# Turned values and keys through DRAM, and sums made by accumulating transfers, in a planned one-core decoder layer

## The chip, the cores and the metric

The kernel runs on one core of one Trainium2 chip. The metric is the device time of one execution in microseconds (us), lower is better. Three timed runs of the kernel before gave 276.04, 276.61 and 276.85 us, so the median is 276.61 us. The engines are named as in the profile: PE does matrix products (and transposes, as products with an identity matrix), DVE works on vectors, ACT evaluates functions and scales, POOL also does vector work and issues transfers, SP only issues transfers.

## The reference, cut to what matters

```python
h = x @ w_in                                  # x: (512, 1024) prompt rows and 8 decode rows
qa, ka, va, za, ga, qb, kb, vb, gb = split(h)
# mixer A, 4 heads, dk=64, dv=128: S_t = diag(a_t) S_{t-1} + k_t^T v_t, o_t = q_t S_t, in chunks
new_state = exp(b_last) * state + einsum('bhsd,bhsv->bhdv', k * exp(b_last - b), v)
# decode rows, one token each: new_state = a * state + k^T v
# mixer B, 8 heads of 64: windows (128,1), (512,4), (2048,16) over past keys, merged by denominators
mix = concat(o_a * silu(ga), o_b * silu(gb))
y = mix @ w_out
out = layer_norm(alpha * x + y, ln_g, ln_b)   # alpha = sqrt(2)
```

Outputs are both groups' rows, the states of mixer A after prompt and decode step, and the new key and value rows. All is float32.

## The kernel before, in words

**Who sets the order.** Every piece of work is a Python generator that yields operations one by one. A planner (class `Plan`, lines 85 to 381, its loop `run` in lines 312 to 334) holds an estimate of every engine's time, takes the generator whose next operation could start first, and among equals the one with the lowest rank, the number given in `add(generator, rank)`. `dense()` at rank 100 is the main stream of projections. What comes out is a fixed order for each engine; on the chip each engine goes through its row in order and waits where an operand isn't there. All instructions are recorded at one line (380 before, 382 in the changed kernel), so groups are told apart by tiles. `SLOTS` and `BANKS` say how many buffers each pool has, `ORDER` in which order the weight groups come, `QUEUE` which engine issues a named kind of transfer ("D" is SP, "G" is POOL).

**Projections.** Every float32 product is made of three passes with operands split into a high and a low part (hi·hi, lo·hi, hi·lo). A weight group has 256 columns. Groups that `token` makes (lines 704 to 721: the values `vb0`, `vb1`, `va0`, `va1`) come for the first two token tiles with features on the partitions (`f`=0, 1; 264 columns, 256 prompt tokens and the 8 decode rows) and for the last two with tokens on the partitions. Attention wants tokens there, so the first half has to be turned. `turn` (730 to 738) does it: a copy to SBUF, two transposes on PE, and a copy from PSUM.

**Keys of mixer A.** `gla_state` (1019 to 1071) makes the decayed keys `kd` (two feature halves, 512 tokens), turns them by eight PE transposes into two PSUM tiles `ps_kt`, copies them to `kt`, and later multiplies `kt` with the values (`ps_kv`).

**Decode state.** `sample_state` (1522 to 1542) works in two halves of four sequences: the old state `s4` comes by SP, ACT multiplies eight 128x128 pieces by the decay, and DVE adds value times key to each (`scalar_tensor_tensor`, 16 in all). SP stores the sum.

**Output.** `out_first` (1764) makes the first two token tiles of the output projection with features on the partitions, four groups g of 256 features. `out_turn` turns them. For g = 3 this is done on PE. For g = 0, 1, 2 the route goes through DRAM: ACT copies `ps_yf` to `feat_y`, DVE turns 32x32 blocks of it into `yw` (`blocks`, 740), POOL stores `yw` to the DRAM tensor `ysc` (`store_blocks`), and POOL loads it back turned into `yx` (`load_turned`). Then `out_evac` (1827) forms y = alpha·y + yx on DVE for token tiles 0 and 1, where y holds the input rows, and takes statistics with `bn_stats` pieces of 256 columns. When all four groups of a tile are in, `norm` (1874) combines statistics, subtracts the mean and multiplies by gamma on DVE, gets 1/sqrt on ACT and DVE, multiplies and adds beta, and stores. Tiles 2 and 3 (`y2`, `y3`) come with tokens on the partitions straight from PE; `y3` is last, and its 512-, 256- and 256-column pieces end the kernel (`last_norm`, 1721). The decode rows have their own small norm (`w_s`, `sums_s`, `residual_sample`), in which PE sums the rows (`ps_ms`, `ps_vs`).

Of the kernel before, what the change touches and what calls it, by code (L numbers as in the profile page):

```python
# [17 lines left out]
ALU = mybir.AluOpType  # L18
# [48 lines left out]
SLOTS = dict(g=23, w=7, r=3, sv=5, pt=2, far=5, tp=2, vp=2, t2=2, st=3, pr=4, t1=5, ob=3, m=6)  # L67
# [11 lines left out]
QUEUE = dict(y="G")  # L79
SLOW, SHARE = 1100, 1.7  # L80

ORDER = "qa0 qb0 qb1 qb2 qb3 kb0 kb1 vb0 kb2 kb3 gb0 vb1 gb1 va0 gb2 gb3 va1 ga0 ga1 ga2 ga3".split()


class Op:
# [3 lines left out]
    def __init__(self, eng, fn, args, kw):  # L89
# [5 lines left out]
        if "accum_out" in kw:  # L95
            self.writes.append(kw["accum_out"])
        if fn == "tensor_tensor_reduce":
            self.writes.append(self.reads.pop())
# [286 lines left out]
def trunk(ctx: ExitStack, tc: tile.TileContext, xT, xp, xs, state, ck, cv, w_in, wab, gnorm,  # L385
# [24 lines left out]
    def rsqrt(o, x, scale, eps, between=None):  # L410
# [4 lines left out]
        if between:  # L415
# [3 lines left out]
            add(between, 5)  # L419
# [284 lines left out]
    def token(g, evac_f, evac):  # L704

        for f in range(2):
# [6 lines left out]
            add(evac_f(ps, f), 61.9)  # L713
# [35 lines left out]
    def load_turned(q, out, sc):  # L749
        return q.dma_start(out, sc.rearrange("k p j -> p k j"))  # L750

# [52 lines left out]
    def dense():  # L804
# [28 lines left out]
        add(gate_decay(pz), 19.1)  # L833
# [10 lines left out]
        add(residual_sample(), 19.7)  # L844
# [82 lines left out]
    def gla_levels():  # L927
# [6 lines left out]
        for li, h in enumerate(LEVELS):  # L934
# [25 lines left out]
            if li % 2:  # L960
                add(gla_level(made), 46.7)
                made = []
# [56 lines left out]
    def gla_state():  # L1019
# [53 lines left out]
    def gla_queries():  # L1073
# [12 lines left out]
        for u in range(2):  # L1086
            yield from make(f"oa{u}", Need("g", f"oa{u}", [P, 2, 512]), 2)
            add(gla_out(u), 13.3 + u)

    def gla_out(u):  # L1090
# [30 lines left out]
        for i in range(2):  # L1121
            add(gla_head(u, i, ps, po), 26 + u + i / 2)
# [17 lines left out]
    def parts(n, own, m, scale):  # L1140

        def evac(ps, u):
# [20 lines left out]
            if n == "k":  # L1163
                add(keys_out(ps, m, u), 9.7)
# [357 lines left out]
    def sample_state():  # L1522
        yield At("vat_out")
        for i in range(2):
# [8 lines left out]
            for bb in range(4):  # L1533
                bi = i * 4 + bb
                for m in range(2):
# [3 lines left out]
            yield D.dma_start(st_s[i * 4 * 256:(i + 1) * 4 * 256, :].rearrange("(b p) v -> p b v", p=P),  # L1539
                              s4.rearrange("p b m v -> p (b m) v"))  # L1540
# [129 lines left out]
    def residual(t):  # L1670
# [7 lines left out]
        yield D.dma_start(y, xp[t * P:t * P + P, :])  # L1678
        mark(f"y{t}")
# [60 lines left out]
    def out_unit(t, c, w, seeded=None):  # L1740
# [16 lines left out]
        if seeded is not None:  # L1757
            add(last_norm(t, ps), 48.2)
        elif w == GW + 2:
            add(early_mean(t, ps), 2)  # L1760
        else:
            add(out_evac(t, c // GW, ps[:, :w]), 2.9)

    def out_first(*units):
# [6 lines left out]
        for (g, f), p in zip(units, ps):  # L1771
            yield from out_half(g, f, p, range(4, KT))
            add(out_turn(g, f, p), 0.3)
# [11 lines left out]
    def out_turn(g, f, ps):  # L1785
        if g == 3:
# [13 lines left out]
            if plan.marks[f"yt_in{g}"] == 2:  # L1800
                plan.share(B[f"yt{g}"], 2)
                for t in range(2):
                    add(out_evac(t, g, B[f"yt{g}"][:, t * GW:t * GW + GW]), 40.9)
# [13 lines left out]
        if plan.marks[f"yt_in{g}"] == 2:  # L1817
# [3 lines left out]
            yx = yield Need("g", f"yx{g}", [P, 2, GW])  # L1821
            yield load_turned(queue["y"], yx.rearrange("p t (k j) -> p (t k) j", j=32), ysc[g])
            plan.share(yx, 2)
            for t in range(2):
                add(out_evac(t, g, yx[:, t]), 2)

    def out_evac(t, g, ps):
# [3 lines left out]
        yield V.scalar_tensor_tensor(y[:, c], y[:, c], ALPHA, ps, op0=ALU.mult, op1=ALU.add)  # L1831
# [201 lines left out]
```

## Time and profile before

| | before |
|---|---|
| median of three timed runs | 276.61 us |
| the profiled execution's own time | 276.23 us |
| its span, first to last instruction | 274.3 us |
| granted PE clock, mean | 0.994 |
| busy: PE / DVE / ACT / POOL | 264.2 / 220.6 / 157.9 / 64.0 us |
| packets moved, bytes | 62999, 54.67 MB |

The profile is one execution. Its time is 1.9 us more than its span, since something lies ahead of the first and behind the last recorded instruction. A row of a group gives engine, operation, output and input by the program's names (buffer numbers left out), shapes, count, then busy time, mean ns of one, idle time ahead of them and who ended most of it. Durations on PE are longer than the distance between starts, since its instructions overlap. The chain of waits is followed back from the last instruction: at each step to what released it.

### The profile page before, as it was taken

The numbers are of one execution on the slowest core, as the hardware profiler recorded it, in microseconds if no ns is written. First come the engines' busy times: TensorE is split into PE (matmuls) and PEld (weight loads), VectorE is DVE, ScalarE is ACT, GpSimd is POOL, SyncE is SP. The second block draws the span as 40 slices with busy tenths as digits, with TensorE's granted clock in tenths as the row PEclk, the third lists the DMA queues.
The fourth block names the chain that finished last, engine by engine and source line by source line (L and its number), as shares of the span: only waits on it lengthen the run. The fifth ranks groups of instructions, "written<-read, shape, count | busy, mean of one in ns | idle before, by whom it ended". The sixth has DMA issues, their size and how long they took to land.

```text
span 274.3 us, 7448 instructions
## 1 busy us (share of the span) xinstructions
PE 264.2 (96%) x2869; PEld 248.9 (91%) x2869; DVE 220.6 (80%) x584; ACT 157.9 (58%) x478; POOL 64.0 (23%) x77
## 2 busy tenths in 40 slices
PE   8999999999799999999999999999999999999990
PEld 5999999899799999989998989999999999998890
DVE  5746789998989799988499954965989898448995
ACT  4727856565457676686464754735589975420221
POOL 3000000000576538220054435353200001330000
PEclk9999999999999999999999999999999999999997
DMA  6978948327959968737599999897952485896142
GB/s 212 342 192 196 301 130 226 81 76 210 307 172 278 236 206 273 194 84 203 153 223 279 282 219 272 217 206 162 244 159 76 114 290 144 228 282 192 58 171 81
DMA packets 62999, 54.67 MB, mean 199 GB/s; under 512 B 13933, under 2 KB 55059, under 8 KB 62965
## 3 DMA queue, kind: packets, MB, share of 16 engines
q1 hardware_dynamic: 61909, 52.18, 69.4%
q0 software_dynamic: 480, 1.57, 2.2%
q8 instruction: 22, 0.36, 0.5%
q10 hardware_dynamic: 576, 0.46, 0.5%
q14 instruction: 12, 0.10, 0.1%
HBM read 47.26 MB, written 7.73 MB: 200 GB/s over the span
## 4 chain that ended last, share of the span: by engine, by line
PE 80%; DMA 8%; DVE 6%; issue 2%; SPq 1%; POOL 0%; ACT 0%; DVEq 0%; POOLq 0%
PE ps_kb L380 9%; PE ps_ga L380 9%; PE ps_gb L380 9%; PE ps_qb L380 9%; PE ps_vb_f L380 4%; PE ps_va_f L380 4%; PE ps_vb L380 4%; PE ps_va L380 4%; PE ps_qa L380 4%; DMA ysc<-yw 4%; PE ps_yf L380 4%; DVE y L380 4%; PE ps_pv L380 3%; PE ps_s L380 3%; PE ps_ka L380 3%; DMA yx<-ysc 3%
## 5 line engine op out<-in xcount | busy, mean ns | idle before, releaser
L380 POOL TENSOR_TENSOR past<-past,qbc 128x256 f32<-128x256 f32 x32 | 29.0, 939 | 86.2 <-DMA qbc<-qsd 77.5
L380 POOL TENSOR_TENSOR vv<-vv,pb 128x256 f32<-128x256 f32 x32 | 26.8, 867 | 48.9 <-DMA pb<-psd_s 43.2
L380 ACT ACTIVATE pr<-pr,ms 128x128 f32<-128x128 f32 (+3 forms) x48 | 23.0, 493 | 7.8 <-DVE ms L380 7.8
L380 ACT COPY pt<-ps_pt 128x256 f32<-128x256 f32 (+1 forms) x29 | 9.8, 347 | 10.4 <-PE ps_pt L380 10.2
L380 DVE CUSTOM_DVE_ANT_0 pr<-ps_s,strip 128x128 f32<-128x128 f32 (+3 forms) x32 | 11.5, 407 | 3.9 <-PE ps_s L380 3.8
L380 ACT ACTIVATE sg<-sg 128x264 f32<-128x264 f32 (+1 forms) x32 | 13.7, 429 | 0.6
L380 PE MATMUL ps_ka<-xx,hi_ka 128*128 128x264 f32 (+1 forms) x64 | 12.2, 283 | 0.0
L380 POOL DMA_DIRECT2D ysc<-yw x3 | 2.5, 818 | 41.0 <-DVE yw L380 40.6
L380 PE MATMUL ps_pt<-cf,pr 128*128 128x128 f32 x56 | 11.3, 274 | 0.0
L380 DVE TENSOR_REDUCE lt<-past 128x8 f32<-128x512 f32 x16 | 10.5, 668 | 0.0
L380 PEld LDWEIGHTS ps_ka<-xx,hi_ka 128*128 128x128 f32 x64 | 9.9, 190 | 0.1
L380 DVE TENSOR_REDUCE o_pv<-vv 128x4 f32<-128x1024 f32 x8 | 9.7, 1206 | 0.0
L380 ACT ACTIVATE d<-d 128x512 f32<-128x512 f32 x11 | 6.6, 641 | 3.9 <-DVE d L380 3.8
L380 PE MATMUL ps_ka<-xx,lo_ka 128*128 128x264 f32 (+1 forms) x32 | 8.7, 283 | 0.0
L380 ACT ACTIVATE qh<-ps_qb 128x128 fp32r<-128x128 f32 x16 | 5.2, 438 | 5.9 <-PE ps_qb L380 5.8
L380 ACT COPY feat_y<-ps_yf 128x256 f32<-128x256 f32 x8 | 3.0, 373 | 8.9 <-PE ps_yf L380 8.9
L380 DVE TENSOR_TENSOR far<-tp,same 128x128 f32<-128x128 f32 (+1 forms) x16 | 8.1, 526 | 0.0
L380 DVE STREAM_TRANSPOSE yw<-feat_y 128x256 f32<-128x256 f32 x6 | 3.8, 640 | 4.8 <-ACT feat_y L380 4.7
L380 PE MATMUL ps_qa<-xx,hi_ka 128*128 128x264 f32 (+1 forms) x32 | 7.4, 304 | 0.1
L380 ACT CAST mhb<-gb 128x256 fp32r<-128x256 f32 x8 | 3.2, 405 | 7.2 <-DVE gb L380 7.2
L380 PEld LDWEIGHTS ps_pt<-cf,pr 128*128 128x128 f32 x56 | 6.9, 140 | 0.3 <-ACT hi_gb__2144 L380 0.2
L380 DVE TENSOR_TENSOR gb<-ps_gb,sg 128x256 f32<-128x256 f32 x8 | 3.4, 419 | 4.4 <-ACT sg L380 4.1
(574 smaller groups left out, 1079.1 us busy)
## 6 DMA issues: line engine op xcount, KB each, us to landing
past<-in_ck_dram SPq DMA_DIRECT2D x8, 512.0 KB, 4.7
vv<-in_cv_dram SPq DMA_DIRECT2D x8, 512.0 KB, 7.2
pb<-psd_s SPq DMA_DIRECT2D x16, 256.0 KB, 7.1
s<-in_state_dram SPq DMA_DIRECT2D x4, 512.0 KB
qbc<-qsd SPq DMA_DIRECT2D x8, 256.0 KB, 5.4
y<-in_xp_dram SPq DMA_DIRECT2D x4, 512.0 KB
x_raw<-in_xT_dram SPq DMA_DIRECT2D x6, 260.0 KB, 5.9
out_dram<-y SPq DMA_DIRECT2D x3, 512.0 KB
```

Of the source, the lines that this page charges most:

```text
L380: getattr(eng.eng, op.fn)(*op.args, **op.kw)
```

## The change

Five things are edited, and nearly every rank is another number.

- **Values of mixer B, first half.** No PE transposes (eight go): `rows_of` copies to SBUF, turns 32x32 blocks on DVE into `vbw`, and after the second feature half SP stores to a DRAM tensor `vsc` and loads back turned into `v0` or `v1`.
- **Decayed keys.** The eight PE transposes and their two ACT copies go. Two DVE block transposes of 128x512 into `kx`, a store to `ksc` and a turned load into `kt`, both issued by POOL.
- **Decode state.** The 16 DVE operations go. ACT multiplies value pieces by the key too (16 more multiplications); SP stores the decayed old state, and POOL adds the products to it in DRAM by an accumulating transfer.
- **Turned outputs.** The load into `yx` and the DVE sum go for g = 0, 1, 2. y0 and y1 are multiplied by alpha once, on ACT, when they are loaded. From `ysc` POOL issues two accumulating transfers per group, one into y0 and one into y1. For g = 3 DVE adds without the factor.
- **Statistics of y2.** DVE's four `bn_stats` and one aggregation become two ACT passes of 1024 columns with accumulated sums (`sq2`, from pool "r").

Pool "w" has 8 buffers for 7 and "sv" 4 for 5; in `ORDER`, `va1` and `gb3` change places.

```diff
-SLOTS = dict(g=23, w=7, r=3, sv=5, pt=2, far=5, tp=2, vp=2, t2=2, st=3, pr=4, t1=5, ob=3, m=6)
+SLOTS = dict(g=23, w=8, r=3, sv=4, pt=2, far=5, tp=2, vp=2, t2=2, st=3, pr=4, t1=5, ob=3, m=6)
-QUEUE = dict(y="G")
+QUEUE = dict(y="G", v="D", k="G")
...
+    def rows_of(g, f, ps):
+        yield from make(f"vbw{g}", Need("g", f"vbw{g}", [P, 2, 2, P])) if f == 0 else iter((At(f"vbw{g}"),))
+        w = B[f"vbw{g}"]
+        feat = yield Need("t1", "feat", [P, GW])
+        yield copy(feat, ps[:, :GW])
+        free(ps)
+        yield blocks(w[:, :, f], feat)
+        free(feat)
+        if f:
+            yield store_blocks(queue["v"], vsc[g], w.rearrange("p t f c -> p (t f) c"))
+            free(w)
+            yield load_turned(queue["v"], B[f"v{g}"][:, :2, :].rearrange("p t (k j) -> p (t k) j", j=32), vsc[g])
+            for _ in range(2):
+                mark(f"vb{g}")
...
+        kx = yield Need("g", "kx", [P, 2, NP])
+        for m in range(2):
+            yield blocks(kx[:, m].rearrange("p (c t) -> p c t", c=TT), kd[:, m])
+        free(kd)
+        yield store_blocks(queue["k"], ksc, kx.rearrange("p m (c t) -> p (m c) t", c=TT))
+        free(kx)
         kt = yield Need("g", "kt", [P, 2, TT, P])
-        for m in range(2):
-            ps = yield bank("t", "ps_kt")
-            for c in range(TT):
-                yield T.transpose(ps[:, c * P:c * P + P], kd[:, m, c * P:c * P + P], ident)
-            yield copy(kt[:, m].rearrange("p c t -> p (c t)"), ps)
-            free(ps)
-        free(kd)
+        yield load_turned(queue["k"], kt.rearrange("p m c (a j) -> p (m c a) j", j=32), ksc)
...
-            ps, raw = yield from turn(ps)
-            free(raw)
-            yield copy(B[f"v{i}"][:, :2, f * P:f * P + P], ps[:, :GW].rearrange("p (t c) -> p t c", t=2))
-            free(ps)
-            mark(f"vb{i}")
+            yield from rows_of(i, f, ps)
...
-                    yield S.mul(s4[:, bb, m, :], s4[:, bb, m, :], a_s[:, m, bi:bi + 1])
-                    yield V.scalar_tensor_tensor(s4[:, bb, m, :], v4[:, bb, m, :], ka_s[:, m, bi:bi + 1], s4[:, bb, m, :],
-                                                 op0=ALU.mult, op1=ALU.add)
...
+            for x, scale in ((s4, a_s), (v4, ka_s)):
+                for bb in range(4):
+                    for m in range(2):
+                        yield S.mul(x[:, bb, m, :], x[:, bb, m, :], scale[:, m, i * 4 + bb:i * 4 + bb + 1])
+                x = x.rearrange("p b m v -> p (b m) v")
+                yield D.dma_start(to, x) if scale is a_s else G.dma_start(to, x, accum_op=ALU.add)
...
-            yx = yield Need("g", f"yx{g}", [P, 2, GW])
-            yield load_turned(queue["y"], yx.rearrange("p t (k j) -> p (t k) j", j=32), ysc[g])
-            plan.share(yx, 2)
             for t in range(2):
-                add(out_evac(t, g, yx[:, t]), 2)
+                yield At(f"y{t}")
+                yield G.dma_start(B["y", t][:, g * GW:g * GW + GW].rearrange("p (k j) -> p k j", j=32),
+                                  ysc[g][8 * t:8 * t + 8].rearrange("k p j -> p k j"), accum_op=ALU.add)
+                add(out_stats(t, g, 1), 9.2)
...
+        if t in (2,):
+            sq = yield Need("r", f"sq{t}", [P, DM])
+            yield S.activation(sq, y, AF.Identity, accum_out=mv[:, 0:1])
+            yield S.mul(mean, mv[:, 0:1], -1.0 / DM)
+            yield S.activation(sq, y, AF.Square, bias=mean, accum_out=mv[:, 1:2])
+            free(sq)
...
-    add(gla_levels(), 20.3)
+    add(gla_levels(), 12.1)
```

**Three places in the new order.** First, POOL's row at the end of the program, before. `vv` and `pb` are past values of the decode rows, `yw0` to `yw2` the turned blocks, `ysc` their DRAM tensors:

```order
L380 TENSOR_TENSOR vv7_3010<-vv7_3010,pb7_3063 128x256 x4
L380 DMA ysc0_95<-yw0_3878 128x4x128
L380 DMA ysc1_96<-yw1_3921 128x4x128
L380 DMA yx0_3918<-ysc0_95 128x16x32
L380 DMA ysc2_97<-yw2_3957 128x4x128
L380 DMA yx1_3953<-ysc1_96 128x16x32
L380 DMA yx2_4004<-ysc2_97 128x16x32
```

POOL's row at the same place in the changed kernel; `out_3_dram` is the decode state in DRAM and `v40`, `v41` are the products of its two halves:

```order
L382 DMA out_3_dram<-v40_3486 128x8x128
L382 DMA ysc0_95<-yw0_3875 128x4x128
L382 DMA ysc1_96<-yw1_3910 128x4x128
L382 DMA y0_3706<-ysc0_95 128x8x32
L382 DMA y1_3708<-ysc0_95 128x8x32
L382 DMA y0_3706<-ysc1_96 128x8x32
L382 DMA y1_3708<-ysc1_96 128x8x32
L382 DMA ysc2_97<-yw2_3952 128x4x128
L382 DMA out_3_dram<-v41_3813 128x8x128
L382 DMA y0_3706<-ysc2_97 128x8x32
L382 DMA y1_3708<-ysc2_97 128x8x32
```

The store of `yw2` stood behind one turned load; now it stands behind four accumulating transfers, which wait for the landings of the first two stores, and the transfer of `v41` stands between it and the last two.

Second, DVE's row near the end, before, with what each instruction waits for (DMASW are POOL's transfers, DMAHW SP's):

```order
L380 SCALAR_TENSOR_TENSOR y2_4042<-y2_4042,ps_y20_4079 128x512 [waits DMAHW1_49,DMASW0_49,PE_49]
L380 BN_STATS stats2_4043<-y2_4042 128x6 [waits DVE_49]
L380 BN_STATS stats2_4043<-y2_4042 128x6
L380 COPY sums_s_85<-ps_ms_4118 64x1 [waits PE_49]
L380 TENSOR_SCALAR w_s_3730<-w_s_3730,sums_s_85 64x128 [waits DVE_49]
L380 SCALAR_TENSOR_TENSOR y0_3726<-y0_3726,yx2_4004 128x256 [waits DMASW5_49]
L380 SCALAR_TENSOR_TENSOR y1_3728<-y1_3728,yx2_4004 128x256
L380 BN_STATS stats0_3727<-y0_3726 128x6 [waits DVE_49]
L380 BN_STATS stats1_3729<-y1_3728 128x6 [waits DVE_49]
L380 BN_AGGR mv0_4152<-stats0_3727 128x2 [waits DVE_49]
```

The same place in the changed kernel:

```order
L382 SCALAR_TENSOR_TENSOR y2_4035<-y2_4035,ps_y20_4068 128x512 [waits DMAHW6_49,PE_49]
L382 COPY sums_s_85<-ps_ms_4105 64x1 [waits PE_49]
L382 TENSOR_SCALAR w_s_3710<-w_s_3710,sums_s_85 64x128 [waits DVE_49]
L382 BN_STATS stats0_3707<-y0_3706 128x6 [waits DMASW3_49]
L382 BN_AGGR mv0_4133<-stats0_3707 128x2 [waits DVE_49]
L382 TENSOR_SCALAR newton_4139<-mv0_4133 128x1 [waits DVE_49]
L382 SCALAR_TENSOR_TENSOR y0_3706<-y0_3706,mv0_4133,gamma_4042 128x1024 [waits DMAHW0_49]
L382 BN_STATS stats1_3709<-y1_3708 128x6 [waits DMASW4_49]
```

DVE's wait for the last load of `yx` has become a wait for the accumulating transfer into y0, at the statistics that stand ahead of all three norms; the statistics of y2 are gone from its row, and the wait for y1 comes behind the first big operation of y0.

Third, PE's row where the decayed keys were turned, before (`ps_kb2_0` is a dense product, `ps_pt31` a turned probability tile):

```order
L380 MATMUL ps_kb2_0_1588<-xx0_132,lo0_kb2__1386 128x264
L380 MATMUL ps_kt_1567<-cf_66,kd_1408 128x128 x4
L380 MATMUL ps_kb2_0_1588<-xx0_132,hi0_kb2__1230 128x264
L380 MATMUL ps_kb2_0_1588<-xx0_133,hi0_kb2__1230 128x264
L380 MATMUL ps_kb2_0_1588<-xx0_132,lo0_kb2__1386 128x264
L380 MATMUL ps_kb2_0_1588<-xx2_215,hi0_kb2__1230 128x264
L380 MATMUL ps_pt31_1584<-cf_66,pr30_1332 128x128 x2
```

And PE's row in the changed kernel where the turned values are first used (`ps_pv00`, the weighted values of mixer B):

```order
L382 MATMUL ps_vb1_2_1968<-hi1_vb1__1734,xx6_309 128x256
L382 MATMUL ps_rows_1987<-cf_66,vnt_82 32x128
L382 MATMUL ps_pv00_2014<-pt00_1284,v0_1364 64x256 x2
L382 MATMUL ps_pv00_2014<-pt10_1473,v0_1364 64x256 x2
L382 MATMUL ps_pv00_2014<-pt00_1284,v0_1364 64x128 x2
L382 MATMUL ps_pv00_2014<-pt10_1473,v0_1364 64x128 x2
L382 MATMUL ps_pt02_2036<-cf_66,pr02_1583 128x128 x2
L382 MATMUL ps_vb1_3_2015<-hi0_vb1__1682,xx0_132 128x256
```

There is no `ps_kt` in the changed row. The first product with `v0` stood within the last third of `kb2`'s first half; now it stands inside `vb1`, 264 dense products behind the end of `vb0`'s feature-major half.

More of the change, by code (lines that the diff above doesn't have):

```diff
@@ L418, in rsqrt @@
             yield S.activation(o, o, AF.Exp, scale=-0.5)
-            add(between, 5)
+            add(between, 24.1)
             yield S.activation(t, o, AF.Square)
@@ L832, in dense @@
         free(zw, *xraw)
-        add(gate_decay(pz), 19.1)
+        add(gate_decay(pz), 41.3)
         yield from make("ka", Need("g", "ka", [P, 2, NP]), 3)
@@ L843, in dense @@
             add(residual(t), 10.3)
-        add(residual_sample(), 19.7)
+        add(residual_sample(), 40.8)
         units = [(g, f) for g in range(4) for f in range(2)]
@@ L960, in gla_levels @@
             if li % 2:
-                add(gla_level(made), 46.7)
+                add(gla_level(made), 62.4)
                 made = []
@@ L1121, in gla_out @@
         for i in range(2):
-            add(gla_head(u, i, ps, po), 26 + u + i / 2)
+            add(gla_head(u, i, ps, po), 51.1 + u + i / 2)
     def gla_head(u, j, ps, po):
@@ L1163, in evac @@
             if n == "k":
-                add(keys_out(ps, m, u), 9.7)
+                add(keys_out(ps, m, u), 56.4)
             else:
@@ L1772, in out_first @@
             yield from out_half(g, f, p, range(4, KT))
-            add(out_turn(g, f, p), 0.3)
+            add(out_turn(g, f, p), 10.7)
     def out_half(g, f, ps, ks):
@@ L1830, in out_evac, with out_stats @@
         c = slice(g * GW, g * GW + size(ps))
-        yield V.scalar_tensor_tensor(y[:, c], y[:, c], ALPHA, ps, op0=ALU.mult, op1=ALU.add)
+        if t < 2:
+            yield V.tensor_tensor(y[:, c], y[:, c], ps, op=ALU.add)
+        else:
+            yield V.scalar_tensor_tensor(y[:, c], y[:, c], ALPHA, ps, op0=ALU.mult, op1=ALU.add)
         free(ps)
-        for i in range(g, g + size(ps) // GW):
-            yield V.bn_stats(st[:, i, :], y[:, i * GW:i * GW + GW])
+        yield from out_stats(t, g, size(ps) // GW)
+    def out_stats(t, g, n):
+        y, st = B["y", t], B["stats", t]
+        for i in range(g, g + n):
+            if t not in (2,):
+                yield V.bn_stats(st[:, i, :], y[:, i * GW:i * GW + GW])
             mark(f"y{t}_done")
```

84 lines of the change are left out of this document (44 added, 40 removed).

## The prediction

> **What bounds the kernel now.** I read the page first (span and busy time), then what PE waits for, then the last 42 us by windows, then the chain of waits and DVE's and PE's timelines at the end. The page's first lines and PE's waits, with the time in total, the times and the longest:
>
> ```profile
> span 274.3 us, 7448 instructions
> PE 264.2 (96%) x2869; PEld 248.9 (91%) x2869; DVE 220.6 (80%) x584; ACT 157.9 (58%) x478; POOL 64.0 (23%) x77
> PE ps_kb L380 <- issue: 1.5, 1, 1.5
> PE warm_ps L380 <- DVE warm L1892: 1.2, 1, 1.2
> PE ps_og L380 <- issue: 0.7, 1, 0.7
> ```
>
> PE is busy 264.2 of 274.3 us. Inside its stream there are two holes worth a name, 1.5 and 0.7 us, and behind neither stands another engine. So time is PE's stream plus what follows its last product. The windows hold length, then busy time (and instructions) of PE, PEld, DVE, ACT and POOL, the granted clock, the DMA share and GB/s:
>
> ```profile
> 232.00:240.00 8.00, 8.00 (x68) 8.00 (x68) 3.29 (x8) 3.29 (x14) 3.19 (x4) 1.00 0.90 239
> 240.00:247.00 7.00, 7.00 (x50) 6.51 (x50) 3.24 (x11) 1.71 (x7) 2.74 (x3) 1.00 1.04 283
> 254.00:261.00 7.00, 7.00 (x33) 5.67 (x32) 6.97 (x17) 1.85 (x11) 0.00 (x0) 1.00 0.18 75
> 261.00:268.00 7.00, 6.61 (x53) 6.27 (x51) 6.93 (x24) 1.83 (x9) 0.00 (x0) 1.00 0.36 150
> ```
>
> From 254 to 268 two engines are full at once: PE without a gap until its end, and DVE 6.97 and 6.93 of 7. In the windows ahead of these the transfers are full instead (0.90 and 1.04). How the two meet, in rows of DVE's, PE's and ACT's timelines (start, length, what):
>
> ```profile
> 251.72 0.13 DVE L380 COPY sums_s<-ps_ms 64x1 f32<-64x1 f32 x1
> 252.70 0.76 DVE L380 SCALAR_TENSOR_TENSOR y<-y,yx 128x256 f32<-128x256 f32 x2 [0.53 <-DMA yx<-ysc]
> 264.95 0.40 DVE L380 SCALAR_TENSOR_TENSOR y<-y,ps_y 128x256 f32<-128x256 f32 x1
> 267.34 1.01 DVE L380 SCALAR_TENSOR_TENSOR y<-y,tail,gamma 128x768 f32<-128x768 f32 x1
> 267.33 0.28 PE L380 MATMUL ps_y<-hi_wo__3598,mla 128*128 128x256 f32 x1
> 267.65 0.47 ACT L380 ACTIVATE sq_y<-ps_y,tail 128x256 f32<-128x256 f32 x1 [5.14 <-PE ps_y L380]
> ```
>
> PE's last product ends at 267.61, and ACT takes it at 267.65. DVE's last wait is for the last turned load, until 252.70; from there it works for 12.25 us without a gap to the sum of `y3`'s third quarter at 264.95, and reaches its 768-wide operation at 267.34. So the end is doubly tight: a shorter PE stream ends the kernel sooner only if DVE's arrival at 252.70 comes sooner too, or its 12.25 us shrink.
>
> **Transposes.** The price on PE, from the chain of waits and the page's group of the like operation:
>
> ```profile
> 85.05 0.22 PE ps_turn L380 x2
> 90.57 0.44 PE ps_kt L380 x4
> L380 PE MATMUL ps_pt<-cf,pr 128*128 128x128 f32 x56 | 11.3, 274 | 0.0
> ```
>
> In the chain four `ps_kt` take 0.44 and two `ps_turn` 0.22, so 0.11 each is what the stream loses. The group's mean of 274 ns is a length, and lengths overlap. Sixteen go: 16 x 0.11 = 1.76 us off the stream. As the upper end, 16 x 0.274 = 4.4. I take 0.11, since PE is gapless there and the chain's pieces add up to the span. By the Trainium skill ("TensorE: Matmul & The Clock Gate", section "Part 4: PE-mode transpose") one transpose costs about 275 ns in a kernel; that is the row's 274, and the sum by it would be 4.4 (rival C).
>
> **What replaces them** must be hidden. First the rows for price and cover: a block transpose on DVE; the landings of the three stores of `yw` (in us, the last number) and of the three turned loads into `yx`; a stretch of the dense stream; where PE uses the keys (`ps_kv`) and the decode rows' products (`ps_sl`); and POOL's last of these products:
>
> ```profile
> 238.73 0.64 DVE L380 STREAM_TRANSPOSE yw<-feat_y 128x256 f32<-128x256 f32 x1 [2.23 <-ACT feat_y L380]
> ysc<-yw POOLq DMA_DIRECT2D x1, 256.0 KB, 5.1
> ysc<-yw POOLq DMA_DIRECT2D x1, 256.0 KB, 2.8
> ysc<-yw POOLq DMA_DIRECT2D x1, 256.0 KB, 5.4
> DMA to landing us min/median/max: 5.8/6.2/7.1
> 39.77 11.85 PE ps_qb L380 x98
> 189.22 1.03 PE ps_kv L380 x32
> 128.77 0.56 PE ps_sl L380 x6
> 115.11 2.98 POOL L380 TENSOR_TENSOR past<-past,qbc 128x256 f32<-128x256 f32 x4 [4.93 <-DVE far L380]
> ```
>
> For the values, the first product with them stands behind 264 dense products; at 11.85 / 98 = 0.12 each that is 31.9 us, against a block transpose, a store and a load: 0.64 + 5.4 + 7.1 = 13.1 us by the slowest of these rows. Costs nothing; if the cover were gone, PE would wait up to 13. For the keys, `ps_kv` comes at 189.22, far behind; `kt` is hidden too.
>
> The key transfers are in POOL's row, the load waiting for the store's landing, with the decode rows' products `past` queued behind. The last of those ended at 118.09, and PE's `ps_sl`, which needs them, starts at 128.77: 10.7 us to spare against a landing of at most 5.4. Nothing again. The value transfers pass through SP's row, whose loads run ahead of use; nothing, with the same 5.4 us as upper end for what waits behind.
>
> **Decode state.** DVE's 16 sums go and ACT gets 16 multiplications:
>
> ```profile
> L380 DVE SCALAR_TENSOR_TENSOR s<-v,ka_s,s 128x128 f32<-128x128 f32 x16 | 5.0, 344 | 0.8 <-ACT s L380 0.8
> 238.66 1.58 ACT L380 ACTIVATE s<-s,a_s 128x128 f32<-128x128 f32 x5
> ```
>
> DVE loses 5.0 us, ACT gains 16 x 0.32 = 5.1; neither was full there (3.29 and 3.24 of DVE, 3.29 and 1.71 of ACT in the windows to 247). Both costs are off the path. The transfer of `v41` (512 KB) isn't: it stands in POOL's row ahead of the last two accumulating transfers and shares the full DMA engines.
>
> **Turned outputs: the term that decides.** POOL's row of before, and how long it took to issue the three turned loads (minimum, median and maximum, ns):
>
> ```profile
> 232.41 0.93 POOL L380 DMA_DIRECT2D ysc<-yw  x1 [38.61 <-DVE yw L380]
> 235.31 0.76 POOL L380 DMA_DIRECT2D ysc<-yw  x1 [1.96 <-DVE yw L380]
> 240.42 1.16 POOL L380 DMA_DIRECT2D yx<-ysc  x1
> 245.59 1.15 POOL L380 DMA_DIRECT2D yx<-ysc  x1 [4.00 <-DMA ysc<-yw]
> L380 POOL DMA_DIRECT2D yx<-ysc x3: 1153/1163/1165, 238.0 to 245.6; - x3
> ```
>
> No accumulating transfer is in this trace. I bound its issue by 0.76 (a store of 512 pieces) and 1.16 (a load of 2048 pieces; an accumulation has 1024) and take 0.9; its landing by 5.8 and 7.1, perhaps 2 us more behind `v41`, and take 6.2. With PE 1.76 sooner: the first store starts at 230.65 and lands at 235.7. Four accumulating transfers follow, 236.2 to 239.8. `yw2` is ready at 238.73 + 0.64 - 1.76 = 237.6, so its store waits 2.2 us for POOL, goes at 239.8 and lands 5.1 later at 244.9. The last pair starts at 245.4, and y0's arrives at **A = 251.6**, about 1.1 ahead of the old 252.70. If the second store lands late (5.4), `yw2` goes at 241.7 and lands at 247.1; with 7.1 and `v41` in front A is 255 to 256.5. If transfers run as fast as the fastest rows, 249.
>
> From A to the sum of `y3` at 264.95 DVE had 12.25 us. Off go the two `yx` sums and `y2`'s statistics; on come waits for ACT:
>
> ```profile
> 253.37 0.75 DVE L380 BATCH_NORM_STATS2 stats<-y 128x6 f32<-128x256 f32 x2
> 258.71 0.75 DVE L380 BATCH_NORM_STATS2 stats<-y 128x6 f32<-128x256 f32 x2
> 260.55 0.26 DVE L380 BATCH_NORM_AGGREGATE mv<-stats 128x2 f32<-128x24 f32 x1
> L380 ACT ACTIVATE d<-d 128x512 f32<-128x512 f32 x11 | 6.6, 641 | 3.9 <-DVE d L380 3.8
> ```
>
> The sums take 252.70 to 253.37, 0.67; the statistics about the same, and their aggregation about 0.2 more: 0.9. That leaves 10.7. ACT's two passes over 1024 columns (641 ns for 512, so about 1.1 each as an estimate) run while DVE centres and scales y1; y0 and y1 now pass one behind the other with their 1/sqrt chains exposed. I add 1.3, bounds 0.6 to 2.1: 12.0, from 11.3 to 12.8. So the sum of `y3` comes at 251.6 + 12.0 = 263.6 against 264.95: 1.35 sooner. PE alone would allow 1.76. The last steps behind it are as before. One place earlier the same queue is in front of PE: statistics of y1 after the second group stand ahead of the reduction that `ps_ms` needs; its transfer, issued by 239, lands at about 245. The copy of PE's sums, 251.72 before, would come at 250.0, and I estimate 2.5 us of DVE's row ahead of it: wanted by 247.5, spare 2.4.
>
> **The sum.** 276.23 (span 274.3 and 1.93 around it) less 1.35 gives 274.9. The median of the three runs lies 0.38 above the profiled execution, so on its scale I forecast 276.61 - 1.3 = **275.3 us**. With A between 250 and 252.4, it runs from 274.8 to 276.0.
>
> The Trainium skill has a rule against this. By its page "SBUF — State Buffer", section "SBUF: two separate sides", descriptors of a transfer issued on GpSimd can't be written while DVE holds the shared port in its two-port mode; in its example 620 ns become about 3100 ("A bandwidth-pool intuition that's wrong"). By that factor, as an estimate, four accumulating transfers would take some 18 us instead of 3.6, if DVE were in that mode all along, and A would come 14 later: a cause for rival A below. The trace doesn't show it: the three turned loads took 1153 to 1165 ns in issue, in windows where DVE was busy 3.2 of 7 or 8 us, so it adds nothing to A's chance.
>
> **The rivals.**
>
> A, slower: the accumulating transfers land late, and DVE stands idle ahead of all three norms. It decides from A = 252.95 (252.95 + 12.0 = 264.95): from there each microsecond of A is one of the end. A = 254.5 gives +1.55, so 278.2; the late sum above, +2 to +3.5. For it: DMA engines at 1.04, the store of `yw2` behind four transfers, `v41` in front, and a read of y that an accumulation needs. Against: the sum leaves 1.35 us of room, and the three groups move the same 768 KB as before. Chance 0.25, half of it within 0.3% of the old time.
>
> B, holes in the new order: nearly every rank differs, so a weight split or a decode product can be late for PE. The old order has holes of 1.5 and 0.7; two more of the larger size give 275.3 + 3.0 = 278.3. For it: in-order rows with new waits on POOL and SP. Against: the spare 10.7 and 18.8 us above. Chance 0.10.
>
> C, faster: a transpose costs PE its whole 274 ns, 16 x 0.274 = 4.4, and DVE's arrival moves along, 272.2. Against: the chain's 0.11. Chance 0.04.
>
> D, no change: the transposes lie in slack, or what is won on PE ends in its holes or at DVE with A = 252.95, 276.6. Against: PE waits at two named places only. Chance 0.05.
>
> **The numbers.** Forecast 0.56 (0.51 faster, 0.05 within), A 0.25 (0.13 within, 0.12 slower), B 0.10 (0.03 within, 0.07 slower), C 0.04 faster, D 0.05 within. "Within" is 0.3%, 0.83 us, about what a measurement of this kernel can tell from no change. Faster 0.55, same 0.26, slower 0.19. Low end: the whole 1.76 and the hole of 0.7 gone, 274.2. High end: A at 254.5, 278.2. Outside lie C, the late end of A and of B and some of the forecast's own tail, 0.18 together.
>
> **What would show it.** Right: PE ends at about 265.9 with no hole above 1 us; the chain has no `ps_kt` and no `ps_turn` ahead of 230; the last accumulation into y0 lands at about 251.6 and DVE's wait before it is under 1 us; the sum of `y3`'s third quarter starts near 263.6. Wrong: DVE idle for over 2 us before the statistics of y0 (A), a new wait of PE (B), an unchanged end with PE 1.76 sooner (D), issues of accumulations longer than 1.2 us on POOL, landings above 7.

## The result and the profile after

The changed kernel is slower: 279.77 us median of nine runs (277.8 to 281.71) against 276.65 of nine runs before (276.04 to 278.48); ratio 1.0102, interval 1.0065 to 1.0140. Its profiled execution took 277.8 us with a span of 276.0. It is the fastest of the nine, so the trace shows less than the median loss: 1.6 us above the profiled execution before. The page's first lines, PE's waits (one more, 1.2 us at `warm_ps`, stands in both kernels), the first of DVE's waits, and the windows of the end (length, then busy time of PE, PEld, DVE, ACT and POOL, granted clock, DMA share, GB/s):

```profile
span 276.0 us, 7420 instructions
PE 263.0 (95%) x2853; PEld 247.1 (90%) x2853; DVE 223.9 (81%) x580; ACT 159.2 (58%) x478; POOL 74.7 (27%) x84
DMA packets 76552, 57.82 MB, mean 209 GB/s; under 512 B 24350, under 2 KB 68548, under 8 KB 76518
```
```profile
PE ps_ms L382 <- issue: 2.6, 1, 2.6
PE ps_oa L382 <- ACT oa L382: 1.1, 1, 1.1
PE ps_pt L382 <- ACT pt L382: 0.5, 1, 0.5
PE ps_ort L382 <- DVE o_r L382: 0.3, 1, 0.3
```
```profile
DVE stats L382 <- DMA y<-ysc: 12.3, 5, 8.1
```
```profile
240.00:247.00 7.00, 7.00 (x44) 6.14 (x43) 0.60 (x2) 0.44 (x2) 4.50 (x4) 1.00 1.47 243
247.00:254.00 7.00, 4.43 (x21) 3.35 (x20) 4.11 (x12) 0.40 (x2) 3.12 (x2) 1.00 1.45 157
254.00:261.00 7.00, 7.00 (x34) 5.63 (x33) 5.70 (x13) 3.62 (x14) 0.00 (x0) 1.00 0.50 93
```

The two old holes of PE are gone; four others stand in their place, 4.5 us against 2.2. The largest, 2.6 us at `ps_ms`, lies in the window from 247, where PE is busy 4.43 of 7. DVE stands idle 12.3 us ahead of statistics, always for a transfer from `ysc` into y. The DMA share is 1.47 and 1.45 from 240 to 254 (1.04 in the fullest window before), while the rate is 243 and then 157 GB/s (283 in that window before): the DMA engines are occupied, but move less. POOL's row shows when these transfers go, DVE's row when they arrive:

```profile
235.36 3.18 POOL L382 DMA_DIRECT2D y<-ysc  x2 [0.98 <-DMA ysc<-yw]
239.00 3.11 POOL L382 DMA_DIRECT2D y<-ysc  x2 [0.46 <-DMA ysc<-yw]
240.76 2.14 POOL L382 DMA_DIRECT2D ysc<-yw  x1
249.96 3.12 POOL L382 DMA_DIRECT2D y<-ysc  x2 [5.46 <-DMA ysc<-yw]
```
```profile
237.04 0.64 DVE L382 STREAM_TRANSPOSE yw<-feat_y 128x256 f32<-128x256 f32 x1
245.76 0.43 DVE L382 BATCH_NORM_STATS2 stats<-y 128x6 f32<-128x256 f32 x1 [8.08 <-DMA y<-ysc]
246.82 0.43 DVE L382 BATCH_NORM_STATS2 stats<-y 128x6 f32<-128x256 f32 x1 [0.64 <-DMA y<-ysc]
247.90 0.43 DVE L382 BATCH_NORM_STATS2 stats<-y 128x6 f32<-128x256 f32 x1 [0.65 <-DMA y<-ysc]
248.99 0.43 DVE L382 BATCH_NORM_STATS2 stats<-y 128x6 f32<-128x256 f32 x1 [0.66 <-DMA y<-ysc]
...
250.95 0.28 DVE L382 TENSOR_REDUCE sums_s<-w_s 64x1 f32<-64x128 f32 x1
...
251.74 0.14 DVE L382 COPY sums_s<-ps_ms 64x1 f32<-64x1 f32 x1
...
254.77 0.43 DVE L382 BATCH_NORM_STATS2 stats<-y 128x6 f32<-128x256 f32 x1 [2.28 <-DMA y<-ysc]
...
266.57 0.40 DVE L382 SCALAR_TENSOR_TENSOR y<-y,ps_y 128x256 f32<-128x256 f32 x1
```

PE's row at its hole, and two pieces of the chain of waits that ended last (start, length, what):

```profile
251.32 0.25 PE L382 MATMUL ps_ms<-sums_s,avg 66*66 66x1 f32 x2 [2.57 <-issue]
240.76 8.91 DMA ysc<-yw
249.96 4.79 DMA y<-ysc
```

A pair of accumulating transfers takes 3.1 to 3.2 us on POOL by its records. But the records overlap: the pair from 239.00 is followed by the store at 240.76, 1.76 us later. The first, issued at 235.36, arrives at 245.76, 10.4 us later, and the next three follow at distances of 1.06 to 1.09 us. `yw2` is ready at 237.68, as forecast, but its store goes at 240.76 and lands 8.9 us later at 249.67. The last accumulation into y0 arrives at 254.77: this is the A of the prediction, 252.70 in the kernel before. The fourth arrival, 248.99, holds back DVE's row up to the sums at 250.95, which PE's `ps_ms` takes at 251.32. (The trace names no engine for this wait; the link is read from the tile `sums_s`.)

### The profile page after: what moved, and what is told of

It is laid out like the page before. It is cut to its first block, busy times and chain, and to the rows that moved or that the text cites. A ratio compares the mean times of both kernels' runs of the same rounds, so it can differ in the third digit from the quotient of the medians.

```text
span 276.0 us, 7420 instructions
## 1 busy us (share of the span) xinstructions
PE 263.0 (95%) x2853; PEld 247.1 (90%) x2853; DVE 223.9 (81%) x580; ACT 159.2 (58%) x478; POOL 74.7 (27%) x84
## 2 busy tenths in 40 slices
DMA packets 76552, 57.82 MB, mean 209 GB/s; under 512 B 24350, under 2 KB 68548, under 8 KB 76518
## 3 DMA queue, kind: packets, MB, share of 16 engines
q0 software_dynamic: 8848, 3.67, 10.5%
## 4 chain that ended last, share of the span: by engine, by line
PE 61%; DVE 18%; DMA 10%; ACT 3%; issue 3%; POOL 2%; SPq 1%; DVEq 0%; POOLq 0%
PE ps_qb L382 9%; PE ps_kb L382 8%; DMA ysc<-yw 5%; PE ps_ga L382 5%; PE ps_vb_f L382 4%; PE ps_gb L382 4%; PE ps_yf L382 4%; PE ps_vb L382 4%; PE ps_qa L382 4%; DVE y L382 3%; PE ps_ka L382 3%; PE ps_va L382 2%; PE ps_va_f L382 2%; PE ps_l L382 2%; PE ps_s L382 2%
## 5 line engine op out<-in xcount | busy, mean ns | idle before, releaser
L382 POOL TENSOR_TENSOR past<-past,qbc 128x256 f32<-128x256 f32 x32 | 27.3, 887 | 82.2 <-DMA qbc<-qsd 71.1
L382 POOL TENSOR_TENSOR vv<-vv,pb 128x256 f32<-128x256 f32 x32 | 27.4, 886 | 55.9 <-DMA pb<-psd_s 35.4
L382 DVE BATCH_NORM_STATS2 stats<-y 128x6 f32<-128x256 f32 x11 | 4.5, 422 | 12.3 <-DMA y<-ysc 12.3
L382 POOL DMA_DIRECT2D y<-ysc x6 | 9.4, 1899 | 6.9 <-DMA ysc<-yw 6.9
L382 ACT COPY pt<-ps_pt 128x256 f32<-128x256 f32 (+1 forms) x23 | 7.7, 348 | 6.2 <-PE ps_pt L382 6.1
L382 POOL DMA_DIRECT2D out_dram<-v x2 | 4.6, 2281 | 21.2 <-DMA w_s<-in_xs_dram 21.2
L382 DVE TENSOR_SCALAR pr<-pr,ms 128x320 f32<-128x320 f32 (+3 forms) x16 | 8.5, 539 | 0.2
L382 PE MATMUL ps_pv<-pt,v 128*64 128x128 f32 (+1 forms) x80 | 6.9, 318 | 0.0
```

The costliest lines, as they stand in the source:

```text
L382: getattr(eng.eng, op.fn)(*op.args, **op.kw)
```

## The experiments

Ratios are to the kernel before, with 95% intervals.

**1. Loads instead of accumulations into y.**

```diff
-            for t in range(2):
-                yield At(f"y{t}")
-                yield G.dma_start(B["y", t][:, ...], ysc[g][...], accum_op=ALU.add)
-                add(out_stats(t, g, 1), 9.2)
+            yx = yield Need("g", f"yx{g}", [P, 2, GW])
+            yield load_turned(queue["y"], yx.rearrange("p t (k j) -> p (t k) j", j=32), ysc[g])
+            plan.share(yx, 2)
+            for t in range(2):
+                add(out_evac(t, g, yx[:, t]), 9.2)
```

> The changed kernel with only the turned outputs undone: a turned load into yx and a DVE sum for each of the three groups, as before; y0 and y1 keep their factor on ACT, all else and all ranks stay. Theory 1 (the six accumulating transfers are what costs, by their own slowness): the loads land 6 to 7 us after issue as they did before, PE has no 2.6 us hole ahead of ps_ms, DVE waits under 1 us for the last one, and the time is 274.5 to 276.0 us, below the kernel before. Rival (SP's 2 MB of loads of y2, y3, gamma and beta, which now start at 234 to 237 instead of 238 to 247, hold up whatever POOL issues): the loads of yx land 9 to 10 us after issue too, the hole ahead of ps_ms stays at 2 us or more, and the time stays at 278 us or above.

Measured: 275.83 us, ratio 0.9965 (0.9939 to 0.9991), faster than before. From the summary of tile `yx`:

```profile
L382 POOL DMA_DIRECT2D yx<-ysc x3: 1153/1166/1171, 236.4 to 249.2; - x3
DMA to landing us min/median/max: 4.3/6.5/8.2
```

The loads land in 6.5 us at the median, and PE's wait at `ps_ms` is gone. So the accumulations into y carry the loss, and the rest of the change leaves a gain of 0.35%, near the forecast's 0.5%. DVE still stands idle 8.0 us for these loads, without a loss: what counts is where the wait stands, not the sum.

**2. The same transfers without the addition.** Same order, instruction for instruction; the residual is missing in these rows.

```diff
-        getattr(eng.eng, op.fn)(*op.args, **op.kw)
+        kw = op.kw
+        if "accum_op" in kw and op.args[0].tensor.space != bass.MemoryType.DRAM:
+            kw = {k: x for k, x in kw.items() if k != "accum_op"}
+        getattr(eng.eng, op.fn)(*op.args, **kw)
```

> The changed kernel, instruction for instruction in the same order, but the six transfers from ysc into y0 and y1 overwrite instead of adding (this leaves the residual out of those rows). Theory 1 (an addition in the transfer is slow by itself): issue falls from 1.5 to 2.2 us to about 1.0, landing from 9 to 10 us to 5 to 7, consecutive ones land less than 1.0 us apart, and the time is 276 us or less. Rival (collision with SP's loads and the place in POOL's row): landings stay at 9 to 10 us and 1.1 us apart, and the time stays between 278 and 281 us.

Measured: 275.92 us, ratio 0.9971 (0.9940 to 1.0002). The page's packet line and the summary of `ysc`, then the same summary of the changed kernel (issue in ns, minimum, median, maximum):

```profile
DMA packets 70599, 57.82 MB, mean 211 GB/s; under 512 B 18205, under 2 KB 62403, under 8 KB 70565
```
```profile
L385 POOL DMA_DIRECT2D y<-ysc x6: 882/892/914, 235.1 to 249.5; - x6
DMA to landing us min/median/max: 3.0/6.6/7.4
```
```profile
L382 POOL DMA_DIRECT2D y<-ysc x6: 1535/1912/2250, 235.4 to 250.8; - x6
DMA to landing us min/median/max: 4.2/8.9/10.5
```

The records of issue are about half as long, and the whole loss is gone. The second pair, the third store, the last pair and the arrival in y0, and the window from 240, in this run:

```profile
239.89 1.75 POOL L385 DMA_DIRECT2D y<-ysc  x2 [3.04 <-DMA ysc<-yw]
241.64 0.77 POOL L385 DMA_DIRECT2D ysc<-yw  x1
248.58 1.80 POOL L385 DMA_DIRECT2D y<-ysc  x2 [4.55 <-DMA ysc<-yw]
251.57 0.43 DVE L385 BATCH_NORM_STATS2 stats<-y 128x6 f32<-128x256 f32 x1 [0.75 <-DMA y<-ysc]
240.00:247.00 7.00, 7.00 (x47) 6.28 (x46) 1.28 (x3) 0.88 (x4) 4.03 (x4) 1.00 1.03 325
```

The last pair arrives 3.0 and 3.6 us after issue instead of 4.8 and 4.9. The third store lands 6.7 us after issue instead of 8.9, so the additions also cost what stands behind them. POOL's row moves no faster with plain writes: the store starts 1.75 us behind the second pair, against 1.76. So the longer records of issue don't hold up the row; what differs is the landings. (The second landing line also counts the three stores into `ysc`, as does the first.) SP's 2 MB of loads of y2, y3, gamma and beta start at 235 to 238 in this kernel too, and POOL's row has the same order, so neither of these alone is the cause. With the addition there are 24350 - 18205 = 6145 more packets under 512 B, which is six transfers of 1024 pieces: each piece of 128 B costs one more packet.

**3. Decode state back on DVE.** The 16 multiplications of `v4` on ACT and the accumulating transfer of 512 KB give way to the old `scalar_tensor_tensor` lines.

> The changed kernel with only the decode state undone: DVE adds value times key, SP stores the sum, no accumulating transfer of 512 KB stands in POOL's row. If that transfer is what delays the last store of yw2 (8.9 us to its landing) and what follows: the store lands in about 5 us, the last accumulation into y0 lands at 250 to 252 instead of 254.8, and the time is 1 to 2 us lower than the changed kernel, 277 to 278.5. If the six accumulations alone are the cause: the wait for y1's second group and the 2.6 us hole ahead of ps_ms stay, and the time stays within 0.7 us of the changed kernel's.

Measured: 281.95 us, ratio 1.0180 (1.0135 to 1.0224), slower still. Both expectations fell. PE's hole at `ps_ms` stays at 2.4 us. The third store lands late without `v41` near it (issued at 238.6, 9.4 us to its landing), so `v41` isn't what makes it late. The new order of DVE's row makes things worse:

```profile
253.98 0.43 DVE L382 BATCH_NORM_STATS2 stats<-y 128x6 f32<-128x256 f32 x1 [1.77 <-DMA y<-ysc]
...
256.20 0.43 DVE L382 BATCH_NORM_STATS2 stats<-y 128x6 f32<-128x256 f32 x1 [1.25 <-DMA y<-ysc]
...
257.03 2.47 DVE L382 SCALAR_TENSOR_TENSOR y<-y,mv,gamma 128x1024 f32<-128x1024 f32 x2
```

Here y1's last arrival stands ahead of both norms, and the first big operation starts at 257.03 instead of 255.60.

**4. Values and keys alone.** The kernel before with `rows_of`, `kx` and `ksc`, and the old ranks.

```diff
-QUEUE = dict(y="G")
+QUEUE = dict(y="G", v="D", k="G")
...
-            ps, raw = yield from turn(ps)
+            yield from rows_of(i, f, ps)
```

> The kernel before with two parts of the change only: first-half values and decayed keys turned by DVE blocks through DRAM, 16 PE transposes gone; ranks, pools and everything else as before. If the price of 0.11 us each holds and the replacement is hidden: PE's stream ends 1.76 us sooner apart from holes, and the time is 274.9 to 276.0 us. If the new path stalls PE (values late): a wait of PE for a DMA or for ps_pv of over 1 us, and 277 us or more. If a transpose is worth its 0.274: 272 us.

Measured: 291.6 us, ratio 1.0525 (1.0483 to 1.0567). The first waits of PE:

```profile
PE ps_pt L380 <- DVE pt L380: 4.9, 1, 4.9
PE ps_yf L380 <- DVE lo_wo__3810 L380: 2.2, 2, 1.9
PE ps_pt L380 <- ACT pt L380: 2.1, 1, 2.1
```

It isn't the values that come late, but other work in rows of the old ranks. In the chain of waits a store of key rows goes from SP at 110.88, lands 3.73 us later and frees what `lo_vb` needs, with `lo_gb`, `far` and `pt` behind it on DVE, until PE goes on at 121.03. Which of the moved instructions sets this off was not taken apart. The new paths and the new ranks belong together.

**5. Store ahead of the second load.** As run 1, and:

```diff
+            mark("y_stored")
+            if g == 1:
+                yield At("y_stored", 3)
             yx = yield Need("g", f"yx{g}", [P, 2, GW])
```

> The changed kernel with turned loads and DVE sums again (as in the first run of the study), and the store of the third group put ahead of the second group's load in POOL's row. In that first run this store stood behind a load that waited for a landing, went at 242.5 though its data was there at 239.7, and DVE's last wait ended at 253.5. If DVE's last wait sets the end (theory): the store goes 2 to 3 us sooner, the last load lands at 250.5 to 252, and the time falls by 0.5 to 1.3 us below that first run, to about 275 us or a ratio near 0.993. If PE alone sets the end there: no change against that run, ratio 0.996 to 0.997.

Measured: 276.11 us, ratio 0.9996 (0.9961 to 1.0030). No gain against run 1; whether a small loss, the intervals don't tell. The store went at 241.15 instead of 242.52.

**6. Run 5 with the decode state on DVE.** No accumulating transfer is left.

> As the run before it in this list, and the decode state back on DVE, so that no accumulating transfer is left in the kernel. If the two 512 KB accumulations cost something where they share the queue with the last load: 0.3 to 1.0 us below the run with them. If DVE's 5 us of sums are what matters when put back behind the turned blocks: equal or up to 1 us above it.

Measured: 277.19 us, ratio 1.0006 (0.9983 to 1.0030). The state's two transfers cost nothing that can be told here, and moving them to DVE gains nothing.

**7. Accumulations with the third store ahead of the second pair.** The same lines as in run 5, in front of the accumulating transfers.

> The changed kernel with all its accumulations, but the store of the third group stands ahead of the second group's two accumulations in POOL's row. If the place in the row is the cause (rival A as forecast): the store lands 2 us sooner, the last accumulation into y0 lands at 252 to 253 instead of 254.8, and the time falls by 1.5 to 2.5 us to about 277.5. If the price of an accumulation is the cause: the second group's lands later by as much, PE's hole ahead of ps_ms stays or grows, and the time stays at 279 us or above.

Measured: 279.26 us, ratio 1.0070 (1.0040 to 1.0100). The place in POOL's row is worth little: PE still waits 2.4 us at `ps_ms`, as the theory of the addition's price said. (The gain of 0.3% on the changed kernel lies within the intervals.) POOL's row and DVE's last two waits:

```profile
237.76 0.79 POOL L382 DMA_DIRECT2D ysc<-yw  x1 [0.39 <-DVE yw L382]
...
247.67 3.09 POOL L382 DMA_DIRECT2D y<-ysc  x2 [4.24 <-DMA ysc<-yw]
```
```profile
253.43 0.43 DVE L382 BATCH_NORM_STATS2 stats<-y 128x6 f32<-128x256 f32 x1 [1.78 <-DMA y<-ysc]
...
255.69 0.43 DVE L382 BATCH_NORM_STATS2 stats<-y 128x6 f32<-128x256 f32 x1 [1.35 <-DMA y<-ysc]
```

The store goes 3.0 us sooner than in the changed kernel; y0's last accumulation arrives 1.3 us sooner. But here y1's last arrival, 255.69, stands ahead of the first big operation, as in run 3.

**8. The planner told of the price.**

```diff
-            self.late = 600 * (rate == 175)
+            self.late = 600 * (rate == 175) + 4000 * ("accum_op" in kw)
```

> The changed kernel with all its accumulations; the planner is only told that an accumulating transfer lands 4 us later than it assumes, so that it may put other work ahead of what waits for one. If the loss is half a matter of the in-order rows (PE's 2.6 us hole ahead of ps_ms, DVE's 8 us wait): the hole goes and the time falls by 1 to 2.5 us, to 277.5 to 278.5. If the landing of the last accumulation sets the end by itself: PE's hole goes but the sum of y3's third quarter stays near 266.6, and the time stays within 0.7 us of the changed kernel's 279.8.

Measured: 278.04 us, ratio 1.0042 (1.0008 to 1.0076). PE's wait at `ps_ms` is gone, and still:

```profile
251.05 3.12 POOL L382 DMA_DIRECT2D y<-ysc  x2 [5.58 <-DMA ysc<-yw]
```
```profile
251.01 0.14 DVE L382 COPY sums_s<-ps_ms 64x1 f32<-64x1 f32 x1
...
266.81 0.41 DVE L382 SCALAR_TENSOR_TENSOR y<-y,ps_y 128x256 f32<-128x256 f32 x1
```

The last pair goes at 251.05, after the sums of `ps_ms`, and the sum of y3's third quarter stays at 266.81. The chain of waits no longer passes through a transfer there: from 225 it follows PE to `ps_vs`, then the decode rows' norm and DVE's new row to the end. The two profiled executions took the same time, 277.88 against 277.80, so no gain shows in the traces. By the ratios of all executions 0.6% go with the order, about half of the 1.3% between the changed kernel and plain writes; but the intervals of this run and the changed kernel overlap slightly (to 1.0076, from 1.0065), so a gain isn't shown.

**9. Accumulations of long pieces.** Same order; each transfer reads 128 pieces of 1 KB, so the turning is left out.

```diff
+        if "accum_op" in op.kw and args[0].tensor.space != bass.MemoryType.DRAM:
+            o, x = args
+            args = (bass.AP(tensor=o.tensor, offset=o.offset, ap=[o.ap[0], [1, GW]]),
+                    bass.AP(tensor=x.tensor, offset=x.offset, ap=[[GW, P], [1, GW]]))
```

> The changed kernel in the same order with all its accumulations, but each of the six takes 128 pieces of 1 KB from DRAM instead of 1024 of 128 B (this leaves out the turning, so the rows of the first two tiles are sums of other places). If the number of pieces sets the price: issue falls from 1.5 to 2.2 us to below 0.8, landing from 9 to 10 us to 4 to 7, and the time is 275.5 to 276.5 as with plain writes (ratio 0.995 to 0.998). If adding itself is slow whatever the pieces, 128 KB for 128 KB: landings stay 1.0 us apart and 9 us or more behind issue, and the time stays at 278 us or above.

Measured: 277.2 us, ratio 1.0004 (0.9976 to 1.0033), between the two expectations:

```profile
DMA packets 71175, 57.82 MB, mean 209 GB/s; under 512 B 18205, under 2 KB 63171, under 8 KB 71141
```
```profile
L387 POOL DMA_DIRECT2D y<-ysc x6: 845/1062/1264, 236.2 to 251.3; - x6
DMA to landing us min/median/max: 3.2/8.1/10.1
```

The small packets are gone and the records of issue nearly fall to those of plain writes; landings fall less. By the ratios about 1.0 of the 1.3% between the changed kernel and plain writes goes with the length of the pieces. The rest may be the addition; its interval meets that of run 2. A plain write of long pieces wasn't run, so what long pieces are worth without an addition isn't known. The profiled execution is one of the longer ones, 277.89 us, and still has a wait of 1.5 us at `ps_ms`.

**10. Run 1 with y2's statistics on DVE.** `bn_stats` and `bn_aggr` for y2 as before.

> Turned loads and DVE sums as in the first run of the study, and the statistics of y2 back on DVE. DVE is full behind its last wait, so if its work there sets the end: 0.9 us of work back gives up to 0.9 us more, ratio 0.997 to 1.000. If the end is PE's: no change, ratio 0.996 to 0.997.

Measured: 275.77 us, ratio 0.9968 (0.9944 to 0.9993), the same as run 1. That part of the change is worth nothing that can be told here. Runs 1 and 10 are the fastest of the study: without accumulations into y the kernel beats both, the one before by 0.3%.

**11. Run 1 with the old ranks of mixer A's outputs.**

```diff
-            add(gla_out(u), 52.2 + u)
+            add(gla_out(u), 13.3 + u)
...
-            add(gla_head(u, i, ps, po), 51.1 + u + i / 2)
+            add(gla_head(u, i, ps, po), 26 + u + i / 2)
```

> Turned loads and DVE sums as in the first run of the study, with the old ranks of mixer A's outputs (gla_out 13.3 and gla_head 26 instead of 52.2 and 51.1), because every kernel with the new ranks shows PE waiting 1.0 to 1.8 us for ACT's oa at 201 to 204. If that hole reaches the end: it goes, and the time falls by 0.5 to 1.3 us, ratio 0.992 to 0.995. If DVE's tail sets the end or the hole only moves: ratio 0.996 to 0.999.

Measured: 275.96 us, ratio 0.9978 (0.9953 to 1.0004), no change against run 1. The hole only moves:

```profile
PE ps_yf L382 <- ACT mhb L382: 1.0, 1, 1.0
```

**12. Run 1 with PE's transposes back.** `turn` and the `ps_kt` lines as before, new ranks.

> Turned loads and DVE sums as in the first run of the study, and first-half values and decayed keys turned on PE again: parts one and two undone, new ranks kept. If the 16 transposes are worth 1.76 us of PE's stream and reach the end: 1 to 2 us above that first run, ratio 1.000 to 1.004. If their removal is worth nothing or the new ranks fit the old paths badly: within 0.7 us, or above 279 us with a new wait of PE.

Measured: 282.3 us, median of three, ratio 1.0216 (1.0170 to 1.0261). That is more than 16 transposes cost even at 0.274 us each (4.4 us, against 6.9 to run 1 by the two ratios). The time is that of the second expectation, above 279 us. Like run 4, it points to ranks and paths that fit each other, and gives no price of a transpose.

## Why the prediction was wrong

**The end is doubly tight: right.** From A to the sum of y3's third quarter the forecast was 12.0 us, 11.3 to 12.8; it was 266.57 - 254.77 = 11.80. The sum came 1.62 us later than before, and the profiled execution's time is 1.57 us longer.

**The step that failed: the accumulating transfers' price.** The prediction put one at 0.9 us of issue, between a store of 512 pieces and a load of 2048, and at 6.2 us to its landing, and let the store behind them land in 5.1. The 0.9 held for POOL's row: each transfer started 0.88 to 0.93 us behind an accumulation ahead of it, though the records of issue last 1.5 to 2.3 us. The landings failed: 8.9 to 10.5 us for the first four, about 1.08 us apart, and 8.9 us for the store of `yw2` behind them (4.8 and 4.9 for the last pair). The upper bound of 7.1 is from rows that only move data. It nearly held for run 2's plain writes (to 7.4), not for transfers that add. Run 2 takes the addition away and nothing else, and the loss goes with it. Taking the state's transfer from the queue (run 3) didn't help, so `v41` was the wrong suspect.

**From 251.6 to 254.77, term by term.** The store of `yw2` went 1.0 us later than forecast, it landed 3.8 us later after its issue (8.9 for 5.1), the last pair followed this landing 0.2 us sooner than assumed, and y0's transfer landed 1.4 sooner (4.8 for 6.2): 3.2 in all. The first of these isn't the additions': with plain writes the store went at 241.64, and POOL waited 3.04 us ahead of the second pair, because the store of `yw1` landed after 5.3 us there (5.1 here), where the sum had 2.8, the fastest row. Run 2's y0 arrives at 251.57, so the forecast's A would have come true without the addition, but in part by luck: this late store is made good by a last landing of 3.0 us.

**The same price one place earlier.** The prediction gave y1's second arrival 2.4 us to spare, 245.1 against 247.5. It came at 248.99, and PE lost 2.6 us at `ps_ms`. In the profiled execution this isn't what set the end: the chain of waits goes from 233.63 through the stores of `yw1` and `yw2`, the last accumulation and DVE's row, and run 8 without the hole took as long. Whether the hole costs time in other executions stays open.

**Rival A is what happened.** Its rule, each microsecond of A past 252.95 is one of the end, gives +1.8 for 254.77; the sum came 1.62 later. Of the reasons given for it, `v41` in front (run 3) and the store's place in POOL's row (run 7, behind two transfers for four) don't carry the loss; the addition itself does. Four of the prediction's five signs of being wrong appeared: DVE idle 2.28 us before y0's statistics, a new wait of PE, records of issue above 1.2 us, and landings above 7. In the median execution the loss is 3.1 us, twice that of the profiled one. No trace shows the other eight, so whether later landings make the difference stays open. Their granted clock, 0.980 to 0.994 on average, doesn't settle it: the profiled execution has 0.990, though each of its windows from 232 to 268 shows 1.00.

**The skill's rule was not the cause.** By the Trainium skill's "SBUF — State Buffer", section "SBUF: two separate sides", DVE would have to hold the port. From 240 to 247 us DVE was busy 0.60 of 7, and there the records of issue were as long as elsewhere; those of plain writes in the same place were little over half.

**Transposes: sign right, size too large.** PE's end less its named waits was 267.61 - 2.2 = 265.4 before and 268.65 - 4.5 = 264.2 after: 1.3 us before rounding, not 1.76. By the same account the traces of the other runs with the new paths and ranks give 0.3 (run 9) to 1.2 (run 11), with 0.9 and 0.6 for runs 8 and 10. All are far below 4.4 us, so rival C falls, and none is nothing, which speaks against D.

**Cover: right, but only with the new ranks.** PE has no wait at `ps_pv`, `ps_kv` or `ps_sl` after. Run 4 shows the same paths losing 14 us under the old ranks. Rival B had a share of its own in the changed kernel, 1.1, 0.5 and 0.3 us of new holes, against the 2.2 that went.

## What to carry to other kernels

An accumulating transfer isn't priced by a load or a store of the same bytes: count its pieces, count what it does to the transfers behind it, and put it only where no engine's row waits soon after. Here folding six sums of 0.4 us into transfers took work from DVE at a place where it waits anyway (8.0 us in run 1, 8.7 with plain writes, 12.3 with accumulations), and made what it waits for come later. If the order is planned, a wrong price can cost twice, once by the late arrival and once by what the plan put behind it; that telling the planner the price wins the second back isn't shown here.

## What was not expected of the hardware

- An addition in a transfer adds one packet under 512 B per piece of 128 B (6145 for 6 x 1024) and makes POOL's record of its issue 1.5 to 2.3 us long instead of 0.9. POOL's next transfer still starts about 0.9 us behind it, as with plain writes. A store behind such transfers took 8.9 us to its landing, against 6.7 behind plain writes.
- While such packets run, the DMA engines look full and move less: share 1.47 at 243 GB/s from 240 to 247, against 1.03 at 325 GB/s in the same window with plain writes.
- In run 4 PE's granted clock fell after PE had been idle for 6 of 30 us. That the idle time brought the fall isn't tested; in the changed kernel PE was idle 2.57 us of the window from 247, at 1.00. In the row of run 4's second window PE is busy all but 1 us, at 0.91:

```profile
90.00:120.00 30.00, 24.05 (x233) 22.46 (x232) 24.82 (x55) 14.74 (x40) 19.72 (x21) 0.98 0.90 241
120.00:150.00 30.00, 28.97 (x278) 26.73 (x279) 21.62 (x81) 17.38 (x57) 3.38 (x5) 0.91 0.68 167
```
